# A weave that keeps TensorE's tile shape, and RWKV state products in 64-column form

## Chip and metric

The kernel runs on one core of one Trainium2 chip. The metric is device time in microseconds, the median of several runs. TensorE (PE) does the matrix products, VectorE (DVE), ScalarE (ACT) and GpSimd (POOL) the rest; SP issues most DMAs.

## What is computed

One decoder layer on 2048 tokens of width 1024. Half of the channels go through 8 RWKV-7 heads, a linear recurrence with a 64×64 state per head, half through 8 heads of dilated attention with three patterns (window 128, 512, 2048 at dilation 1, 4, 16). Their outputs are joined, projected, normalised, and go through a mixture of experts. The change is in the part that does RWKV and attention:

```
def step(state, inp):
    r_t, w_t, k_t, v_t, a_t, b_t = inp
    sa = einsum('bhvk,bhk->bhv', state, a_t)
    state = state * w_t + sa[..., None] * b_t + v_t[..., None] * k_t
    y_t = einsum('bhvk,bhk->bhv', state, r_t)
    return state, y_t
...
for window, dil in ((128, 1), (512, 4), (2048, 16)):
    o, l = dilated_branch(q, k, v, rel_bias, window, dil)
...
mix = concatenate([y_rwkv, y_att], -1) @ w_o
```

## The kernel before

The stages follow one another: `project` (input projections and the RWKV inputs), `mixers` (RWKV and attention), `mix_out` (output projection, first norm, router), then the experts. Neighbouring stages overlap at their edges.

In `mixers`, RWKV works in chunks of 128 tokens, two chunks and two heads (one pair, number u) at a time: 16 rounds, each with two pairs i = 0, 1. A round has four parts. `rwkv_front` multiplies triangles (L650, row tiles of 64 rows), cuts out 16×16 blocks, sends them through DRAM to another layout, inverts them on VectorE in 15 steps (L691, L692), sends them back, and GpSimd spreads them into the tile U (L703). `rwkv_inverse` doubles the inverse: products in 128×128 (L742, L748), 32×32 (L756, L766) and 64×64 tiles (L774, L778, L788), then WF (L797). `rwkv_state` makes L822, L834, L849, L858 (128×64 tiles), and then for each chunk c the new state (L875: MK·vt, L877: E·st, both full 128×128 products, of which only the two 64×64 diagonal blocks are kept) and the output (L886 in 128×64 tiles, L888 in 128×128).

Attention runs 12 passes (4 head pairs × 3 patterns) of 16 blocks, dealt to three streams. A block makes scores (L1066 with two key blocks, L1069 with one), adds bias and takes the extreme on VectorE (L1079, L1082), exponentials on ScalarE (L1085), transposes on TensorE (L1091), copies them out (L1095, L1097), and multiplies by V (L1105, 128×64 tiles). When a head pair's three patterns are done, `attn_combine` writes their statistics to DRAM, reads them back in another layout, makes factors, writes and reads these, scales and adds the three outputs (L1213, L1160) and writes y (L1217). `heads(0)` of `mix_out` then loads y (L1313).

All of these are generators, eight and more streams. They yield what they are about to do: an engine and an estimated time (`_pe(430)`), or None where they wait for another stream. `weave` keeps a clock for each engine and for each stream, finds the streams' possible starts, and takes, among those within SLACK = 100 ns of the first, one that `late()` names as being in a hurry, then the lowest number:

```
first = min(starts)[0]
hurry = late()
t, i = min((x for x in starts if x[0] <= first + SLACK), key=lambda x: (x[1] not in hurry, x[1]))
```

So the weave sets the order in which the program is written. In this kernel that is not yet the order on the engines: the recording layer's own scheduler orders each engine's instructions again, except inside `manual_schedule`, where the named engine keeps the order as written. `project` and `mix_out` do that for TensorE, `mixers` does not. At run time every engine takes its instructions in its fixed order.

A matmul has a tile shape, rows × columns of the array that it uses; the profile writes it as 128\*128, 64\*128, 128\*64, 64\*64, 32\*32. An fp32 matmul shows as two records (passes), a transpose and an fp32r matmul as one.

Of the kernel before, what the change touches and what calls it, by code (L numbers as in the profile page):

```python
# [12 lines left out]
AF = mybir.ActivationFunctionType  # L13
# [5 lines left out]
P = 128  # L19
# [37 lines left out]
SLACK = 100.0  # L57
# [5 lines left out]
FRONTS = 2  # L63
HEAD = 10
LATENCY = 100.0
CDEC = math.exp(-0.5)
NEG = -1e30
PATTERNS = (1, 4, 16)
# [48 lines left out]


def _act(n):
    return "ACT", 190 + 0.56 * n  # L120


def _dve(n):
    return "DVE", 60 + 1.06 * n


def _pool(n):
    return "POOL", 100 + 2.2 * n


def _pe(ns):
    return "PE", ns


def _wait(ns):
    return "DMA", ns


def weave(streams, late=lambda: ()):

    clock, now = {}, 0.0
    ready = [0.0] * len(streams)
    pend = [next(g, False) for g in streams]
    while True:
        starts = []
        for i, g in enumerate(streams):
            if pend[i] is None:
                pend[i] = next(g, False)  # L150
                if pend[i]:
                    ready[i] = max(ready[i], now)
            if pend[i]:
                starts.append((max(clock.get(pend[i][0], 0.0), ready[i]), i))
        if not starts:
            assert not any(x is None for x in pend)
            return
        first = min(starts)[0]
        hurry = late()
        t, i = min((x for x in starts if x[0] <= first + SLACK), key=lambda x: (x[1] not in hurry, x[1]))  # L160
        eng, ns = pend[i]
        if eng != "DMA":
            clock[eng] = t + ns
        ready[i] = now = t + ns + LATENCY
        pend[i] = next(streams[i], False)


class K:
# [483 lines left out]
    def rwkv_front(self, n, pps, last):  # L652

        nc, kp = self.nc, self.rf
# [4 lines left out]
        self.busy = True  # L659
        C, Dg = T("C", [P, 2, 4, 32], 1), T("Dg", [P, 2, 4, 16], 1)  # L660
        AB = T("AB", [P, 2, 2, 2, P], ROUNDS)
        yield _pe(900)
        pa = [self.rps[0].tile([P, BT], F32, name="ps0", tag="ps0").rearrange("p (a c s) -> p a c s", a=2, c=2) for _ in range(2)]
        for i, pp in enumerate(pps):
            self.triangles([pa[h][:, i] for h in range(2)], pp, 0)
# [40 lines left out]
    def rwkv_inverse(self, i, pp):  # L706
# [6 lines left out]
            yield None  # L713
        AB, ta = pp["AB"], pp["ta"]
        AW = T("AW", [P, 2, 2, 192])
        yield _pe(500)
        pa = [ps()[:, 0:2 * P].rearrange("p (c s) -> p c s", c=2) for _ in range(2)]
        self.triangles(pa, pp, 1)
        for h in range(2):
# [28 lines left out]
            mm(p2[:, h, c], X[:, h, c], t1[:, h, c], start=True, stop=True)  # L748
        yield _dve(4 * P)
        nc.vector.copy_predicated(U4, self.mask("lv16", 4), p2.rearrange("p h c s -> p (h c) s"))  # L750
        yield _pe(430)
        halves = [(slice(d, d + 32), slice(d + 32, d + 64)) for d in (0, 64)]
        p1 = ps().rearrange("p (h c s) -> p h c s", h=2, c=2)
        for r1, r2 in halves:
# [4 lines left out]
        yield _act(240)  # L759
        for r1, r2 in halves:  # L760
            nc.scalar.copy(t1[r1, :, :, 0:32], p1[r1, :, :, 0:32])
        yield _pe(430)
        p2 = ps().rearrange("p (h c s) -> p h c s", h=2, c=2)
        for r1, r2 in halves:
            for h, c in pairs:
# [2 lines left out]
        for r1, r2 in halves:  # L768
            nc.scalar.copy(U[r1, :, :, r2], p2[r1, :, :, 0:32])
        lo, hi = slice(0, 64), slice(64, 128)  # L770
        yield _pe(250)
        px = ps().rearrange("p (h c s) -> p h c s", h=2, c=2)
        for h, c in pairs:
            nc.tensor.transpose(px[0:64, h, c, 0:64], U[lo, h, c, lo], self.c("eye")[lo, lo])  # L774
        yield _pe(460)
        p1 = ps().rearrange("p (h c s) -> p h c s", h=2, c=2)
        for h, c in pairs:
            mm(p1[lo, h, c, lo], AB[hi, h, c, lo], U[hi, h, c, hi], start=True, stop=True)  # L778
# [3 lines left out]
        yield _act(256)  # L782
        t6 = t1[lo, :, :, lo]
        nc.scalar.copy(t6, p1[lo, :, :, lo])
        yield _pe(460)
        p2 = ps().rearrange("p (h c s) -> p h c s", h=2, c=2)
        for h, c in pairs:
            mm(p2[lo, h, c, lo], X6[:, h, c], t6[:, h, c], start=True, stop=True)  # L788
# [14 lines left out]
    def rwkv_state(self, i, u, q, pp):  # L803
# [13 lines left out]
        yield _pe(950)  # L817
# [36 lines left out]
        yield _pe(700)  # L854
# [12 lines left out]
        for c in range(2):  # L867
            first = q == 0 and c == 0
            last = q == 7 and c == 1
            st, after = (self.state[u][(c + n) % 2] for n in range(2))  # L870
            if not last:
                yield _pe(224 if first else 448)
                pn = ps()[:, 0:P]

                mm(pn, MK[:, c], vt[:, c], start=True, stop=first)  # L875
                if not first:
                    mm(pn, E[:, c], st, start=False, stop=True)  # L877
                yield _act(64)
                rho = self.rho[:, u, q + c, 1 - c:2 - c]
                nc.scalar.activation(after[H[0], H[0]], pn[H[0], H[0]], AF.Copy, scale=rho[H[0]])  # L880
                yield _dve(64)
                nc.vector.tensor_scalar_mul(after[H[1], H[1]], pn[H[1], H[1]], rho[H[1]])
            yield _pe(640)
            py = ps()[:, 0:P]
            for h in range(2):
                mm(py[H[h]], vt[:, c, H[h]], MJ[:, h, c], start=True, stop=first)  # L886
            if not first:
                mm(py, st, Q[:, c], start=False, stop=True)  # L888
            yield _act(128)
            nc.scalar.copy(yt[:, col[c]], py)  # L890
        nc.sync.dma_start(self.y[u * P:(u + 1) * P, q * 2 * P:(q + 1) * 2 * P], yt)
# [2 lines left out]
    def mixers(self, attention=True):  # L894
# [12 lines left out]
        def fronts(s):  # L907
            for n in range(s, len(rounds), FRONTS):
                if n in begun:
                    yield from begun[n]  # L910
                    continue
                while n >= ROUNDS and not all("done" in pp for pp in pps[n - ROUNDS]):
                    yield None
                load(n)
                yield _wait(2500)
                yield from self.rwkv_front(n, pps[n], pps[n - 1])

        def inverses(i):
            for n in range(len(rounds)):
                yield from self.rwkv_inverse(i, pps[n][i])  # L920

        def states(i):
            for n, (q, u) in enumerate(rounds):
                yield from self.rwkv_state(i, u + i, q, pps[n][i])
                self.steps[0] += 1

        with ExitStack() as es:
            att = []
            self.rwkv_setup(es)
            self.busy = False  # L930
# [12 lines left out]
            def late():  # L943

                return range(4 + FRONTS, 8 + FRONTS) if self.steps[1] < (self.steps[0] + HEAD) * PACE else (4 + FRONTS,)

            weave([states(0), states(1), inverses(0), inverses(1), *(fronts(s) for s in range(FRONTS)), *att], late)


    def attn_bias(self, tile, bank):  # L950
# [24 lines left out]
    def attn_streams(self):  # L975
# [71 lines left out]
        def blocks(s, k):  # L1047
            hp, n = passes[k]
            for blk in range((s - k) % 3, 16, 3):
# [50 lines left out]
                yield _pe(550 if two else 275)  # L1100
                o = po[:, at % 2]
                for b in kb:
                    vb = V[:, prev if b == 0 else blk]
# [889 lines left out]
```

## Time and profile before

| | |
|---|---|
| median of 3 runs | 3265.83 us (3265.79 to 3274.77) |
| the profiled execution | 3262.19 us, its span 3260.4 us |
| busy share of the span | PE 90%, DVE 65%, ACT 47%, POOL 21% |
| mean granted TensorE clock | 0.934 |
| HBM | 163 GB/s over the span |

The profile is of one execution. PE's ends are modelled, so the start of the next instruction tells more than an end. The mixers take about 806 to 1815 us of the span.

### The profile page before, as it was taken

The numbers are of one execution on the slowest core, as the hardware profiler recorded it, in microseconds if no ns is written. First come the engines' busy times: TensorE is split into PE (matmuls) and PEld (weight loads), VectorE is DVE, ScalarE is ACT, GpSimd is POOL, SyncE is SP. The second block draws the span as 40 slices with busy tenths as digits, with TensorE's granted clock in tenths as the row PEclk, the third lists the DMA queues.
The fourth block names the chain that finished last, engine by engine and source line by source line (L and its number), as shares of the span: only waits on it lengthen the run. The fifth ranks groups of instructions, "written<-read, shape, count | busy, mean of one in ns | idle before, by whom it ended". The sixth has DMA issues, their size and how long they took to land. (4 is left out here: it accounts for less than half of the span.)

```text
span 3260.4 us, 49197 instructions
## 1 busy us (share of the span) xinstructions
PE 2938.1 (90%) x16686; PEld 2343.0 (72%) x16687; DVE 2118.0 (65%) x4730; ACT 1529.3 (47%) x3650; POOL 675.4 (21%) x682
## 2 busy tenths in 40 slices
PE   7989888999798999998998799899999999998880
PEld 6666777777676777777786577788777777776660
DVE  4997333786654766655757688653577777766756
ACT  3434212554444544543543333311477777765642
POOL 0442000344100211111202122223011111112216
PEclk9999999999898988998897999999999999999985
DMA  5213433788615335234214453243599999987846
GB/s 172 74 59 99 107 81 80 215 273 267 139 55 127 94 74 129 72 95 104 75 31 130 144 183 123 97 138 89 181 298 322 326 301 324 315 296 220 293 129 209
DMA packets 364061, 533.04 MB, mean 163 GB/s; under 512 B 92376, under 2 KB 204640, under 8 KB 363792
## 3 DMA queue, kind: packets, MB, share of 16 engines
q1 hardware_dynamic: 330144, 459.09, 44.1%
q0 software_dynamic: 14496, 45.93, 6.0%
q10 hardware_dynamic: 19168, 24.86, 3.1%
q8 instruction: 133, 2.18, 0.3%
q14 instruction: 120, 0.98, 0.1%
HBM read 402.27 MB, written 128.06 MB: 163 GB/s over the span
## 5 line engine op out<-in xcount | busy, mean ns | idle before, releaser
L1708 DVE TENSOR_TENSOR wl<-raw,wh 128x512 fp32r<-128x512 f32 x768 | 478.3, 681 | 88.4 <-ACT wh L1707 87.7
L1707 ACT CAST wh<-raw 128x512 fp32r<-128x512 f32 x768 | 417.3, 620 | 13.2 <-DMA raw<-in_w_up_dram 12.1
L198 PE MATMUL ps<-xh,wh 128*128 128x512 f32 x640 | 262.6, 410 | 1.1 <-ACT xh L322 1.0
L199 PE MATMUL ps<-xl,wh 128*128 128x512 f32 x640 | 258.7, 404 | 1.2 <-DVE xl L323 1.2
L200 PE MATMUL ps<-xh,wl 128*128 128x512 f32 x640 | 258.2, 403 | 0.0
L1085 ACT ACTIVATE pe<-pe,ms 128x256 f32<-128x256 f32 (+1 forms) x384 | 174.8, 457 | 144.0 <-DVE ms L1082 133.0
L1837 POOL DMA_INDIRECT acc<-ysb,ix x48 | 95.8, 1996 | 623.0 <-ACT ysb L1836 403.0
L198 PE MATMUL pe<-wh,XX 128*128 128x512 f32 x480 | 199.8, 416 | 3.8 <-ACT wh L1707 3.8
L199 PE MATMUL pe<-wl,XX 128*128 128x512 f32 x480 | 192.0, 400 | 2.6 <-DVE wl L1708 2.6
L200 PE MATMUL pe<-wh,XX 128*128 128x512 f32 x480 | 190.9, 398 | 0.0
L198 PEld LDWEIGHTS ps<-xh,wh 128*128 128x128 f32 x640 | 124.7, 195 | 34.6 <-issue 2.6
L199 PEld LDWEIGHTS ps<-xl,wh 128*128 128x128 f32 x640 | 124.7, 195 | 30.1 <-DVE xl L323 2.4
L200 PEld LDWEIGHTS ps<-xh,wl 128*128 128x128 f32 x640 | 124.1, 194 | 29.5
L1091 PE MATMUL pl<-eye,pe 128*128 128x128 f32 x600 | 126.3, 299 | 10.7 <-ACT pe L1085 9.6
L1066 PE MATMUL pl<-KK,Q 128*128 128x256 f32 x432 | 115.4, 393 | 15.6 <-DMA KK<-ks 8.0
L198 PE MATMUL pb<-gh,XH 128*128 128x512 f32 x320 | 126.1, 394 | 0.0
L199 PE MATMUL pb<-gl,XH 128*128 128x512 f32 x320 | 125.2, 391 | 0.0
L1752 PE MATMUL pe<-wh,XX 128*128 128x512 f32 x288 | 120.1, 417 | 5.4 <-ACT wh L1707 5.4
L200 PE MATMUL pb<-gh,XL 128*128 128x512 f32 x320 | 124.9, 390 | 0.0
L1105 PE MATMUL po<-pe,V 128*64 128x128 f32 x1200 | 119.4, 300 | 3.6 <-DVE O L1117 3.2
L1753 PE MATMUL pe<-wl,XX 128*128 128x512 f32 x288 | 118.8, 413 | 2.9 <-DVE wl L1708 2.9
L1082 DVE CUSTOM_DVE_ANT_0 pe<-pl,bias 128x256 f32<-128x256 f32 x216 | 82.6, 418 | 59.7 <-PE pl L1066 37.4
(418 smaller groups left out, 7627.5 us busy)
## 6 DMA issues: line engine op xcount, KB each, us to landing
raw<-in_w_gate_dram SPq DMA_DIRECT2D x128, 512.0 KB
raw<-in_w_up_dram SPq DMA_DIRECT2D x128, 512.0 KB
raw<-in_w_down_dram SPq DMA_DIRECT2D x128, 512.0 KB
pk<-pk SPq DMA_DIRECT2D x32, 512.0 KB
pk_t<-pk SPq DMA_DIRECT2D x32, 512.0 KB
KK<-ks SPq DMA_DIRECT2D x64, 256.0 KB
wr<-in_w_in_dram SPq DMA_DIRECT2D x48, 256.0 KB
rkk<-rkk SPq DMA_DIRECT2D x32, 384.0 KB
```

Of the source, the lines that this page charges most:

```text
L198: mm(out, lh, rh, start=first, stop=False)
L199: mm(out, lh, rl, start=False, stop=False)
L200: mm(out, ll, rh, start=False, stop=last)
L1066: mm(pl[:, h], q, toks(KK[:, m, h], n, prev, 2), start=m == 0, stop=m == 1)
L1085: nc.scalar.activation(pe[:, h, w], pe[:, h, w], AF.Exp, bias=m_[h], scale=-1.0, accum_out=s_[h])
L1091: nc.tensor.transpose(pt[:, h, b], pe[:, h, b * P:(b + 1) * P], self.c("eye"))
L1105: mm(o[h * 64:(h + 1) * 64, j], vb[:, h * 64:(h + 1) * 64], tt[:, h, b], start=b == kb[0], stop=b == 1)
L1707: nc.scalar.copy(wh[:, c], raw[:, c])
L1708: nc.vector.tensor_tensor(out=wl[:, c], in0=raw[:, c], in1=wh.bitcast(F32)[:, c], op=ALU.subtract)
L1752: mm(ps, L[:, 0:P], wh, start=first, stop=False)
L1753: mm(ps, L[:, 0:P], wl, start=False, stop=last)
L1837: nc.gpsimd.indirect_dma_start(out=self.acc, out_offset=bass.IndirectOffsetOnAxis(ap=ix[0:r, e, b:b + 1], axis=0), in_=ysb[0:r], in_offset ...
```

## The change

The pieces now also say the tile shape that they use (`_pe(430, 32)`; 128 is the full array, 1 stands for 64×128, 2 for 128×64). The weave remembers the shape in use, counts 190 ns for a change, lets a TensorE piece of the same shape be taken up to KEEP = 600 ns after the first possible start, and prefers such pieces to a hurry. The weave runs inside `manual_schedule` for TensorE. And four products of `rwkv_state` are written as pairs on 128×64 tiles: the state in two 64-column halves (pn is 64 columns wide), the output's Q product by halves of its rows.

```diff
-    return "ACT", 190 + 0.56 * n
+    return "ACT", 190 + 0.56 * n, 0
...
-def _pe(ns):
-    return "PE", ns
+def _pe(ns, mode=128):
+    return "PE", ns, mode
...
 def weave(streams, late=lambda: ()):
-    clock, now = {}, 0.0
+    clock, now, tile_ = {}, 0.0, 128
...
-        t, i = min((x for x in starts if x[0] <= first + SLACK), key=lambda x: (x[1] not in hurry, x[1]))
-        eng, ns = pend[i]
+        other = lambda i: pend[i][0] == "PE" and pend[i][2] != tile_
+        t, i = min((x for x in starts if x[0] <= first + (SLACK if other(x[1]) or pend[x[1]][0] != "PE" else KEEP)), key=lambda x: (other(x[1]), x[1] not in hurry, x[1]))
+        eng, ns, mode = pend[i]
+        if eng == "PE":
+            ns += CHANGE * other(i)
+            tile_ = mode
...
             if not last:
-                yield _pe(224 if first else 448)
-                pn = ps()[:, 0:P]
-                mm(pn, MK[:, c], vt[:, c], start=True, stop=first)
+                yield _pe(110 if first else 220, 2)
+                pn = ps()[:, 0:64]
+                for h in range(2):
+                    mm(pn[H[h]], MK[:, c, H[h]], vt[:, c, H[h]], start=True, stop=first)
                 if not first:
-                    mm(pn, E[:, c], st, start=False, stop=True)
+                    for h in range(2):
+                        mm(pn[H[h]], E[:, c, H[h]], st[:, H[h]], start=False, stop=True)
                 yield _act(64)
...
-            yield _pe(640)
+            yield _pe(220 if first else 440, 2)
             py = ps()[:, 0:P]
             for h in range(2):
                 mm(py[H[h]], vt[:, c, H[h]], MJ[:, h, c], start=True, stop=first)
             if not first:
-                mm(py, st, Q[:, c], start=False, stop=True)
+                for h in range(2):
+                    mm(py[H[h]], st[:, H[h]], Q[:, c], start=False, stop=True)
...
-            weave([states(0), states(1), inverses(0), inverses(1), *(fronts(s) for s in range(FRONTS)), *att], late)
+            with self.tc.manual_schedule(engines={mybir.EngineType.PE}):
+                weave([states(0), states(1), inverses(0), inverses(1), *(fronts(s) for s in range(FRONTS)), *att], late)
```

Lines move by 8 to 12 in the changed code: L650 becomes L658, L742 L750, L875 and L877 become L884 and L887, L886 and L888 become L896 and L899, L1066 and L1069 become L1078 and L1081, L1091 becomes L1103, L1105 L1117, L1217 L1229.

Three places in TensorE's order. First the opening of the stage, up to the first product with an inverse U. In the kernel before (the rows just ahead of it; L1091 transposes, L1105 attention products, L1066 scores):

```order
L1105 MATMUL po<-pe_7672,V 64x128 x4
L1066 MATMUL pl_7736<-KK,Q 128x256 x4
L1105 MATMUL po<-pe_7661,V 64x128 x4
L1066 MATMUL pl_7781<-KK,Q 128x256 x4
L1091 MATMUL pl_7789<-eye,pe_7741 128x128 x2
L742 MATMUL ps_7582<-U_7219,AB 128x128 x4
```

and in the changed one (L1117 products, L1078 scores, L1103 transposes, L750 the product with U):

```order
L1117 MATMUL po<-pe_7349,V 64x128 x2
L1117 MATMUL po<-pe_7356,V 64x128 x4
L1117 MATMUL po<-pe_7369,V 64x128 x4
L1078 MATMUL pl_7519<-KK,Q 128x256 x4
L1078 MATMUL pl_7526<-KK,Q 128x256 x4
L1078 MATMUL pl_7533<-KK,Q 128x256 x4
L750 MATMUL ps_7541<-U_7219,AB 128x128 x4
L1103 MATMUL pl_7548<-eye,pe_7524 128x128 x4
```

Of the attention products (L1105, now L1117), 42 stood ahead of the first product with U, and 10 do now: the three rows here are all of them.

Second a state update in the middle. Before (L858 gives E and Q; L875, L877 the state; L886, L888 the output):

```order
L1091 MATMUL pl_12533<-eye,pe_12338 128x128 x4
L875 MATMUL ps_11623<-vt_11263,MK_11201 128x128
L877 MATMUL ps_11623<-S_7124,E_7132 128x128
L849 MATMUL ps_11879<-RB_11333,WF_11678 128x192 x2
L849 MATMUL ps_11884<-RB_11333,WF_11678 128x192 x2
L742 MATMUL ps_11627<-U_11549,AB 128x128 x4
L1105 MATMUL po<-pe_12355,V 64x128 x4
L1066 MATMUL pl_12619<-KK,Q 128x256 x4
L1066 MATMUL pl_12635<-KK,Q 128x256 x3
L886 MATMUL ps_11638<-MJ_11200,vt_11263 64x128 x2
L888 MATMUL ps_11638<-Q_11612,S_7124 128x128
L858 MATMUL ps_11904<-RB_11333,WF_11678 64x192 x4
```

and changed:

```order
L866 MATMUL ps_12292<-RB_11776,WF_12207 64x192 x4
L866 MATMUL ps_12301<-RB_11839,WF_12215 64x192 x4
L884 MATMUL ps_12309<-vt_11903,MK_11778 64x64 x2
L887 MATMUL ps_12309<-S_7128,E_7132 64x64 x2
L1117 MATMUL po<-pe_12112,V 64x128 x2
L884 MATMUL ps_12323<-vt_11934,MK_11841 64x64 x2
L887 MATMUL ps_12323<-S_7130,E_7133 64x64 x2
L896 MATMUL ps_12329<-MJ_11777,vt_11903 64x128 x2
L899 MATMUL ps_12329<-Q_12306,S_7128 64x128 x2
L884 MATMUL ps_12338<-vt_11903,MK_11778 64x64 x2
L887 MATMUL ps_12338<-S_7129,E_7132 64x64 x2
L896 MATMUL ps_12344<-MJ_11840,vt_11934 64x128 x2
```

All twelve rows of the second piece have one tile shape, 128×64; the first piece changes shape five times.

Third the end of the stage. Before, the last attention product and the start of the RWKV matmuls that follow it, 227 in number with the first ones of `mix_out` among them:

```order
L766 MATMUL ps_15680<-t_15546,X_15545 32x32 x8
L1105 MATMUL po<-pe_17036,V 64x128 x4
L774 MATMUL ps_16114<-eye,U_15603 64x64 x4
L778 MATMUL ps_16120<-U_15603,AB 64x64 x4
L774 MATMUL ps_15701<-eye,U_15543 64x64 x4
```

Changed, the last RWKV matmuls and the start of the 234 attention matmuls that follow them:

```order
L896 MATMUL ps_16745<-MJ_16354,vt_16488 64x128 x2
L899 MATMUL ps_16745<-Q_16715,S_7131 64x128 x2
L1081 MATMUL pl_16752<-KK,Q 128x256 x2
L1103 MATMUL pl_16757<-eye,pe_16656 128x128 x2
L1117 MATMUL po<-pe_16656,V 64x128 x2
```

Attention ended first and now ends last; the combine of the last head pair follows it in both.

## Rows read from the trace of the kernel before

**Rows 1.** busy time by stretch: us, busy us by engine, granted clock, DMA

```profile
806.00:1717.00 911.00, 854.95 (x6853) 689.98 (x6851) 546.27 (x2029) 431.50 (x1488) 135.79 (x250) 0.92 0.38 92
1717.00:1815.00 98.00, 72.94 (x436) 57.09 (x436) 65.78 (x138) 33.46 (x81) 23.64 (x15) 0.72 0.56 157
```

**Rows 2.** waits of TensorE from 810 to 1717 us, longest in total

```profile
PE ps L858 <- DVE AW L721: 14.6, 2, 9.2
```

**Rows 3.** timeline of TensorE: start us, us, engine, line, operation, out<-in, form, records

```profile
1644.05 1.16 PE L742 MATMUL ps<-U,AB 128*128 128x128 f32 x8
1645.14 0.44 PE L886 MATMUL ps<-MJ,vt 128*64 128x128 f32 x4
...
1701.19 0.44 PE L1105 MATMUL po<-pe,V 128*64 128x128 f32 x4
1701.56 0.66 PE L834 MATMUL ps<-eye,pk_t 128*128 128x128 f32 x4
...
1702.64 0.66 PE L1105 MATMUL po<-pe,V 128*64 128x128 f32 x8
1703.23 1.71 PE L650 MATMUL ps<-pk_t 64*128 64x128 f32 x16
```

**Rows 4.** timeline of TensorE around one state update

```profile
1640.12 0.39 PE L875 MATMUL ps<-vt,MK 128*128 128x128 f32 x2
1640.34 0.39 PE L877 MATMUL ps<-S,E 128*128 128x128 f32 x2
1640.66 0.44 PE L1105 MATMUL po<-pe,V 128*64 128x128 f32 x4
1641.03 1.31 PE L1066 MATMUL pl<-KK,Q 128*128 128x256 f32 x4
1642.27 0.43 PE L1105 MATMUL po<-pe,V 128*64 128x128 f32 x2
```

**Rows 5.** timeline of the weight loads there

```profile
1640.23 0.30 PEld L877 LDWEIGHTS ps<-S,E 128*128 128x128 f32 x2
1640.66 0.20 PEld L1105 LDWEIGHTS po<-pe,V 128*64 128x64 f32 x4
```

**Rows 6.** timeline of the opening, TensorE, then GpSimd (POOL)

```profile
843.91 0.66 PE L1105 MATMUL po<-pe,V 128*64 128x128 f32 x8
...
850.33 0.44 PE L1091 MATMUL pl<-eye,pe 128*128 128x128 f32 x2 [3.71 <-ACT pe L1085]
...
871.89 0.66 PE L1105 MATMUL po<-pe,V 128*64 128x128 f32 x8
...
874.21 1.06 PE L742 MATMUL ps<-U,AB 128*128 128x128 f32 x8
...
872.76 2.51 POOL L703 TENSOR_TENSOR U<-ct,Vc 128x512 f32<-128x512 f32 x2 [1.87 <-DMA Vc<-inv]
```

**Rows 7.** timeline of VectorE and ScalarE between scores and products

```profile
1702.43 0.42 DVE L1082 CUSTOM_DVE_ANT_0 pe<-pl,bias 128x256 f32<-128x256 f32 x1
...
1703.55 0.51 ACT L1085 ACTIVATE pe<-pe,ms 128x256 f32<-128x256 f32 x1
...
1707.75 0.59 ACT L1095 COPY pe<-pl 128x512 f32<-128x512 f32 x1 [0.93 <-PE pl L1091]
```

**Rows 8.** timeline of the end: TensorE, SP's DMA issues, TensorE

```profile
1716.97 0.66 PE L1105 MATMUL po<-pe,V 128*64 128x128 f32 x8 [0.28 <-ACT pe L1095]
...
1767.72 5.66 SPq L1217 DMA_DIRECT2D y<-O  x2
1773.42 0.43 SPq L1313 DMA_DIRECT2D y<-y  x1
...
1815.41 0.58 PE L198 MATMUL pa<-woh,YH 128*128 128x512 f32 x1
```

**Rows 9.** busy time by stretch, two neighbours

```profile
1151.00:1157.90 6.90, 6.90 (x41) 5.73 (x40) 4.27 (x16) 2.95 (x14) 1.20 (x3) 1.00 0.14 20
1157.96:1171.61 13.65, 13.65 (x60) 11.05 (x60) 6.07 (x18) 3.55 (x13) 4.35 (x11) 0.50 0.24 69
```

More of the change, by code (lines that the diff above doesn't have):

```diff
@@ L65 @@
 LATENCY = 100.0
+CHANGE = 190.0
+KEEP = 600.0
 CDEC = math.exp(-0.5)
@@ L119, in _act @@
 def _act(n):
-    return "ACT", 190 + 0.56 * n
+    return "ACT", 190 + 0.56 * n, 0
 def _dve(n):
-    return "DVE", 60 + 1.06 * n
+    return "DVE", 60 + 1.06 * n, 0
 def _pool(n):
-    return "POOL", 100 + 2.2 * n
-def _pe(ns):
-    return "PE", ns
+    return "POOL", 100 + 2.2 * n, 0
+def _pe(ns, mode=128):
+    return "PE", ns, mode
 def _wait(ns):
-    return "DMA", ns
+    return "DMA", ns, 0
 def weave(streams, late=lambda: ()):
-    clock, now = {}, 0.0
+    clock, now, tile_ = {}, 0.0, 128
     ready = [0.0] * len(streams)
@@ L661, in rwkv_front @@
         AB = T("AB", [P, 2, 2, 2, P], ROUNDS)
-        yield _pe(900)
+        yield _pe(900, 1)
         pa = [self.rps[0].tile([P, BT], F32, name="ps0", tag="ps0").rearrange("p (a c s) -> p a c s", a=2, c=2) for _ in range(2)]
@@ L715, in rwkv_inverse @@
         AW = T("AW", [P, 2, 2, 192])
-        yield _pe(500)
+        yield _pe(500, 1)
         pa = [ps()[:, 0:2 * P].rearrange("p (c s) -> p c s", c=2) for _ in range(2)]
@@ L750, in rwkv_inverse @@
         nc.vector.copy_predicated(U4, self.mask("lv16", 4), p2.rearrange("p h c s -> p (h c) s"))
-        yield _pe(430)
+        yield _pe(430, 32)
         halves = [(slice(d, d + 32), slice(d + 32, d + 64)) for d in (0, 64)]
@@ L761, in rwkv_inverse @@
             nc.scalar.copy(t1[r1, :, :, 0:32], p1[r1, :, :, 0:32])
-        yield _pe(430)
+        yield _pe(430, 32)
         p2 = ps().rearrange("p (h c s) -> p h c s", h=2, c=2)
@@ L770, in rwkv_inverse @@
         lo, hi = slice(0, 64), slice(64, 128)
-        yield _pe(250)
+        yield _pe(250, 64)
         px = ps().rearrange("p (h c s) -> p h c s", h=2, c=2)
@@ L774, in rwkv_inverse @@
             nc.tensor.transpose(px[0:64, h, c, 0:64], U[lo, h, c, lo], self.c("eye")[lo, lo])
-        yield _pe(460)
+        yield _pe(460, 64)
         p1 = ps().rearrange("p (h c s) -> p h c s", h=2, c=2)
@@ L784, in rwkv_inverse @@
         nc.scalar.copy(t6, p1[lo, :, :, lo])
-        yield _pe(460)
+        yield _pe(460, 64)
         p2 = ps().rearrange("p (h c s) -> p h c s", h=2, c=2)
@@ L816, in rwkv_state @@
         MJ, MK = T("MJ", [P, 2, 2, P]), T("MK", [P, 2, P])
-        yield _pe(950)
+        yield _pe(950, 1)
         prs = [ps().rearrange("p (c k s) -> p c k s", c=2, k=2) for _ in range(2)]
@@ L853, in rwkv_state @@
             nc.vector.tensor_tensor(out=MK[:, :, H[h]], in0=pm[h][:, :, P:192], in1=MK[:, :, H[h]], op=ALU.add)
-        yield _pe(700)
+        yield _pe(700, 2)
         pq = ps()[:, 0:384].rearrange("p (c s) -> p c s", s=192)
@@ L871, in rwkv_state @@
             if not last:
-                yield _pe(224 if first else 448)
-                pn = ps()[:, 0:P]
-                mm(pn, MK[:, c], vt[:, c], start=True, stop=first)
+                yield _pe(110 if first else 220, 2)
+                pn = ps()[:, 0:64]
+                for h in range(2):
+                    mm(pn[H[h]], MK[:, c, H[h]], vt[:, c, H[h]], start=True, stop=first)
                 if not first:
-                    mm(pn, E[:, c], st, start=False, stop=True)
+                    for h in range(2):
+                        mm(pn[H[h]], E[:, c, H[h]], st[:, H[h]], start=False, stop=True)
                 yield _act(64)
                 rho = self.rho[:, u, q + c, 1 - c:2 - c]
-                nc.scalar.activation(after[H[0], H[0]], pn[H[0], H[0]], AF.Copy, scale=rho[H[0]])
+                nc.scalar.activation(after[H[0], H[0]], pn[H[0]], AF.Copy, scale=rho[H[0]])
                 yield _dve(64)
-                nc.vector.tensor_scalar_mul(after[H[1], H[1]], pn[H[1], H[1]], rho[H[1]])
-            yield _pe(640)
+                nc.vector.tensor_scalar_mul(after[H[1], H[1]], pn[H[1]], rho[H[1]])
+            yield _pe(220 if first else 440, 2)
             py = ps()[:, 0:P]
@@ L1099, in blocks @@
                     yield None
-                yield _pe(550 if two else 275)
+                yield _pe(550 if two else 275, 2)
                 o = po[:, at % 2]
```

## The prediction

> **What bounds the kernel now.** I read the page's busy shares first, and they put TensorE far ahead of every other engine. The change touches one stage, the mixers, so I then read the busy time by stretch [rows 1]. The mixers hold TensorE from about 806 us, where the first RWKV matmuls come in, to 1815 us, where the output projection flows. That is two stretches. Until 1717 us, where the last attention product runs, TensorE is busy for 854.95 of 911 us at a granted clock of 0.92. In the 98 us after it, it is busy for 72.94 us at 0.72. The first stretch is bound by TensorE's own issue, the second by latency. The waits of TensorE in the first stretch add up to some 55 us, the largest group 14.6 in two waits [rows 2], so most of it is not waiting. What does it spend on?
>
> The timeline of TensorE answers. The product line L1105 (128\*64 tiles) runs with 4 records, and the next line starts 0.37 us later; with 8 records the next starts 0.59 us later [rows 3]. Four records more cost 0.22 us, 0.055 each, so a section of one tile shape has a fixed cost of 0.37 − 0.22 = 0.15 us, paid at the change of shape. Where the shape stays (L877 after L875), two records take 0.22 us with no such gap; when L1105 follows L877, it starts 0.32 us after L877 instead of 0.22 [rows 4]. So 0.10 of the 0.15 us lies ahead of the new section, 0.05 in its first weight load.
>
> **The change, part by part.**
>
> *Fewer changes of shape.* Counted along TensorE's order as built, from the first RWKV matmul to the last of the stage: 991 changes of tile shape before, 338 now. In the stretch before either order's end piece (below) it is 950 against 316. 634 fewer × 0.15 us = **−95 us**. Nothing hides this cost, since TensorE is the engine that is waited for. The low bound is the gap alone, 0.10 × 634 = 63 us. The high one comes from L742: eight records and 1.09 us to the next line [rows 3], 8 × 0.11 and 0.21 more, so 133 us. I take 0.15, as L1105 is the commonest section. [...] The weight load of L1105 starts with its matmul, at 1640.66 us, 0.43 us behind the first load for L877, which stood 0.11 us ahead of its own matmul [rows 4, 5]; across a change the pull-ahead is not there, and the measurement decides for 0.15.
>
> *State products.* The new state of a chunk was one 128-column product MK·vt and one E·st (L875, L877), four records of 0.11 us [rows 4]. Now each is two 64-column products side by side on 128\*64 tiles (L884, L887). No row shows that form. The nearest, L1105 with 128 columns, takes 0.055 us a record with two side by side [rows 3]; with half the columns, half of that, and twice the records: 8 × 0.027 = 0.22 us for 0.44. 56 such pairs: **−12 us**. If the records do not shrink with their columns, 8 × 0.055 = 0.44 us and nothing is won, which is the other end. The output's second product (L888, now L899) keeps 2 × 0.11 us as 4 × 0.055; splitting it saves only changes, counted above.
>
> *The opening.* The order is now the weave's own, and TensorE can't pass a wait. The first RWKV product that needs the inverse U (L742, now L750) ran at 874.21 us, right behind the U that GpSimd wrote from 872.76 us [rows 6]. Ahead of it stood 42 attention products; now there are 10. U comes through three DMA round trips and is not made earlier by this change. So TensorE has 32 products, eight blocks of two keys, less to fill that wait: a block is 4 scores, 4 transposes and 4 products, about 0.11 to 0.13 us each, plus three changes, 1.8 us. **+15 us** (0 if U comes that much earlier, 20 with the clock at half for part of it).
>
> *Shorter distances.* Pieces of one shape now stand together, so scores, transposes and products of three attention streams come in threes and a block's own next step stands closer behind. From a block's scores to its transposes, VectorE and ScalarE need from 1702.43 to 1704.06 us [rows 7]; I count against 1.5 us, since the first head's transposes need not wait for the second. From transposes to products it is a copy of 0.59 us [rows 7] and the hand-over on either side, an estimated 0.85. I added up the work that stands between in the new order, with the durations above: it is under 1.5 us ahead of the transposes for 22 of 192 blocks, and under 0.85 us ahead of the products for 43. The missing time sums to 29 us; in the old order, by the same count, to 2. A wait of one stream covers that of its neighbours, but a crowded ScalarE lengthens the need. **+20 us** (0 to 60).
>
> *The end.* Before, attention ended first: its last product at 1716.97 us, its combine (statistics out to memory and back, factors out and back) beside the last RWKV round, the last y written from 1767.72, the first load of the next stage at 1773.42, the projection flowing at 1815.41 us [rows 8]. Now RWKV ends first, and 234 attention matmuls in 26 blocks stand behind it, and behind these the combine with nothing beside it. The 26 blocks have 41 us of matmuls and changes, with the strided scores at (1.24 − 0.15)/4 = 0.27 us [rows 4]; nearly alone, from the products at 843.91 to those at 871.89 us, eight more blocks of two keys took 28 us, 3.5 us each [rows 6]. 12 of the 26 have two keys, 14 have one and half the work: 12 × 3.5 + 14 × 1.75 = 66 us. The combine and first loads took 98 us from the last product; 56 of it up to 1773.42, in which VectorE and SP also served RWKV, so I take 40, and 26 of the 42 behind it: 66. Together 132 us for 98: **+34 us** (9, if the blocks run at 41, to 60). The RWKV work that stood there, 45 us with its changes, is about what the attention rest is, so the sums match.
>
> Sum against the profiled execution, 3262.19 us (span 3260.4): −95 − 12 + 15 + 20 + 34 = −38, **3224 us**. The median of the three runs is 3265.83, 3.6 us above that execution; I leave the sum where it is.
>
> **The rivals.**
>
> *The covers hold.* TensorE stays fed as before and the end is no longer than now: 3262 − 107 = 3155 us. For it: DVE at 546 and ACT at 432 of 911 us [rows 1] have room; the U of all later rounds now stands further behind its triangles. Against it: the end piece is plain in the order. Chance 0.16.
>
> *The fixed order waits.* This is the one on the other side. TensorE in the weave's order waits at scores → transposes → products because the three streams arrive together, and nothing may pass. It decides where the added wait per block exceeds (38 + 20)/192 = 0.30 us; at 0.5 us, a third of the chain of [rows 7], it is 96 us instead of 20, so 3224 + 76 = 3300 us. For it: at 850.33 TensorE waited 3.71 us for ScalarE with attention nearly alone [rows 6]. Against it: between 874 and 1717 such waits are rare [rows 2]. Chance 0.18.
>
> *The clock falls more.* [...] Chance 0.06.
>
> *It does nothing.* The changes of shape are not what TensorE spends on, since something else paces it: 3262 us. Against it: [rows 3, 4]. Chance 0.05.
>
> **How the numbers follow.** My forecast has 0.55, and its own range goes from 3180 to 3255. The range takes in the covers case with changes at 0.15, the bounds of the end, and most of the waiting case: 3155 to 3295. A measurement of this kernel tells 0.3% (10 us) from no change. Faster by more: 0.55 + 0.16 = 0.71. Within: 0.06 + 0.05 = 0.11. Slower: 0.18.
>
> **What would show it.** Right: TensorE's records between 874 us and RWKV's end in about 95 us less time; lines L884 to L899 as one section; a wait of over 15 us ahead of the first L750; a stretch of about 65 us with attention lines alone, then about 65 us nearly empty of matmuls. Wrong: if sections with the same records still cost 0.15 us where the shape stays; if waits at L1103 and L1117 add up to over 60 us (second rival); if the end piece is under 100 us (first rival).

## The result, and the profile after

The changed kernel takes 3375.31 us (median of 4 runs, 3371.83 to 3381.03), the kernel before beside it 3265.81 us: ratio 1.0332, 95% interval 1.0310 to 1.0354. By that ratio it is slower by 108 us. The forecast was 3224 us, the range 3155 to 3295. The profiled execution took 3371.83 us, its span is 3370.0 us.

The busy time by stretch of the changed kernel answers to [rows 1] (us, then busy us of PE, its weight loads, DVE, ACT, POOL, then the granted clock, the DMA share and GB/s). The stretches are RWKV to its end, the attention rest, and the combine with the first loads of the next stage.

```profile
806.00:1773.00 967.00, 776.64 (x7303) 669.37 (x7301) 541.32 (x1977) 414.17 (x1408) 138.16 (x253) 0.85 0.36 87
1773.00:1853.00 80.00, 58.90 (x318) 39.34 (x316) 30.04 (x133) 35.48 (x134) 0.24 (x1) 0.71 0.21 59
1853.00:1925.00 72.00, 13.56 (x33) 8.09 (x30) 34.53 (x58) 16.41 (x27) 18.02 (x12) 0.51 0.60 163
```

Ahead of RWKV's end TensorE now idles for 967 − 777 = 190 us where it idled for 56, and the granted clock is 0.85 for 0.92.

To compare whole stages, I cut each execution at 806 us and at 1470 us before the end of its span; what follows the second cut is the experts and the end of the projection. Two rows give that stretch, for the kernel before and then for the changed one:

```profile
806.00:1790.40 984.40, 917.22 (x7244) 741.02 (x7243) 597.75 (x2139) 458.69 (x1551) 155.34 (x260) 0.90 0.39 96
```

```profile
806.00:1900.00 1094.00, 836.42 (x7618) 708.96 (x7616) 591.38 (x2144) 458.55 (x1551) 153.53 (x261) 0.82 0.36 89
```

By these cuts the two stretches differ by as much as the spans, 1094.0 − 984.4 = 109.6 us. That nothing is lost behind them is seen at the last product of the output projection, which stands 1191 us ahead of the end of the span before and 1189 after. I split the stretch in three: **idle** is the length less PE's busy time; the **half-clock cost** is half of PE's busy time inside the stretches granted 0.50 (before 170 us busy in 198 at 0.50, after 268 in 390); **work** is the rest, busy time as at full clock (in the kernel before, eight records of L822 take 1.08 us to the next line at 1100.98 us, granted 1.00, and 2.01 us at 826.89, granted 0.50). Before: 67 idle, 85 half clock, 832 work. After: 258, 134, 702. So work fell by 130 us, more than the 107 of the forecast, idle time rose by 190 and the half-clock cost by 49.

The work that went is to be seen where the 128\*64 sections now run into each other (timeline of TensorE, answering to [rows 3, 4]):

```profile
1396.51 0.64 PE L1117 MATMUL po<-pe,V 128*64 128x128 f32 x8
1396.95 0.31 PE L884 MATMUL ps<-vt,MK 128*64 128x64 f32 x4
...
1398.05 0.48 PE L896 MATMUL ps<-MJ,vt 128*64 128x128 f32 x4
1398.27 0.48 PE L899 MATMUL ps<-Q,S 128*64 128x128 f32 x4
```

Eight records take 0.44 us to the next line, four 0.22, with nothing between: 0.055 a record, and no 0.15 us.

The idle time is to be seen in TensorE's costliest groups from 806 to 1925 us (busy us, mean ns, idle before them and what ended it):

```profile
L1103 PE MATMUL pl<-eye,pe 128*128 128x128 f32 x600 | 119.2, 317 | 28.3 <-ACT pe L1097 23.9 <-DVE ms L1094 1.7 <-DVE Dg L686 0.8
L1117 PE MATMUL po<-pe,V 128*64 128x128 f32 x1200 | 109.6, 307 | 65.1 <-ACT pe L1107 18.8 <-DVE O L1129 18.3 <-DVE O L1131 15.1
...
L658 PE MATMUL ps<-pk_t 64*128 64x128 f32 x512 | 53.5, 305 | 31.3 <-DVE MJ L835 13.3 <-DVE MK L861 4.9 <-DVE AW L729 4.5
```

Attention's transposes and products, L1103 and L1117, wait 93 us, 72 of it ahead of RWKV's end; RWKV's first product L658 waits 31 us, nearly all of it for VectorE, whose lines L835, L861 and L729 read the ps tiles that TensorE wrote before. The longest of these waits, in the timeline of TensorE, VectorE and ScalarE:

```profile
1031.42 0.66 PE L1117 MATMUL po<-pe,V 128*64 128x128 f32 x8
1042.95 0.19 DVE L1172 TENSOR_TENSOR mn<-stt 128x32 f32<-128x32 f32 x1 [14.89 <-DMA stt<-stat]
...
1043.84 0.28 ACT L1181 ACTIVATE f<-f 128x96 f32<-128x96 f32 x1 [12.48 <-DVE f L1172]
1044.03 0.57 ACT L1107 COPY pe<-pl 128x512 f32<-128x512 f32 x1
1044.65 1.12 PE L1117 MATMUL po<-pe,V 128*64 128x128 f32 x8 [12.58 <-ACT pe L1107]
```

VectorE waits 14.9 us for a DMA of the combine, ScalarE 12.5 us for VectorE, the copy L1107 starts 0.19 us behind ScalarE's L1181, and TensorE waits 12.6 us for the copy. None of the three engines has a record inside its wait, so this one fault stops all three. TensorE's records stand in the order as built: at the opening 20 of L1117 from 854.04 us, 12 of L1078 from 855.28, then L750 after a wait of 12.70 us, with L1103's transposes behind it.

This fault is not what the change brought. The kernel before has it too:

```profile
1049.24 0.19 DVE L1160 TENSOR_TENSOR mn<-stt 128x32 f32<-128x32 f32 x1 [11.87 <-DMA stt<-stat]
...
1049.99 0.80 PE L877 MATMUL ps<-S,E 128*128 128x128 f32 x2 [7.37 <-DVE E L862]
```

Up to the end of the first of the two, attention or RWKV, TensorE's waits at these stops add up to 22 us before (7.4, 5.4 and 9.2; the last two are the 14.6 of [rows 2]) and to 21 us now (12.6 and 8.5). What is new are other and mostly shorter waits. From 900 us, behind the opening, TensorE waits 37 us to 1717 in the kernel before and 148 us to RWKV's end now. Two rows of the waits in that stretch now (us in total, times, longest), then the one that answers to them before:

```profile
PE po L1117 <- DVE O L1129: 18.3, 12, 8.6
...
PE po L1117 <- DVE O L1131: 12.2, 10, 3.2
```

```profile
PE po L1105 <- DVE O L1117: 2.8, 2, 2.0
```

L1129, L1131 and L1133 copy attention's finished products out of PSUM, and the next products wait for that: 33 us for 3. With the stops at the combine left out, these waits rise by 112 us, in the main: +30 here, +18 where attention's transposes and products wait for ScalarE, and +65 where RWKV's lines wait for VectorE (+49) and ScalarE (+16).

The end answers to [rows 8] (TensorE, SP's DMA issues, TensorE):

```profile
1852.41 1.12 PE L1117 MATMUL po<-pe,V 128*64 128x128 f32 x8 [0.73 <-ACT pe L1107]
...
1893.37 4.98 SPq L1229 DMA_DIRECT2D y<-O  x2
1898.40 0.43 SPq L1325 DMA_DIRECT2D y<-y  x1
...
1901.61 0.76 PE L1334 MATMUL pa<-y,ct 128*128 128x256 f32 x1 [47.73 <-DMA y<-y]
```

The combine now has nothing beside it: TensorE waits 47.7 us in one piece.

### The profile page after: what moved, and what is told of

The parts are those of the page before. It is cut to its first block, busy times and chain, and to the rows that moved or that the text cites. A ratio compares the mean times of both kernels' runs of the same rounds, so it can differ in the third digit from the quotient of the medians.

```text
span 3370.0 us, 49843 instructions
## 1 busy us (share of the span) xinstructions
PE 2863.6 (85%) x17038; PEld 2314.6 (69%) x17039; DVE 2111.3 (63%) x4730; ACT 1529.9 (45%) x3650; POOL 673.1 (20%) x682
## 5 line engine op out<-in xcount | busy, mean ns | idle before, releaser
L1117 PE MATMUL po<-pe,V 128*64 128x128 f32 x1200 | 109.6, 307 | 65.1 <-ACT pe L1107 18.8
L1103 PE MATMUL pl<-eye,pe 128*128 128x128 f32 x600 | 119.2, 317 | 28.3 <-ACT pe L1097 23.9
L1117 PEld LDWEIGHTS po<-pe,V 128*64 128x64 f32 x1200 | 71.1, 148 | 90.9 <-ACT pe L1107 24.6
L1103 PEld LDWEIGHTS pl<-eye,pe 128*128 128x128 f32 x600 | 79.4, 157 | 55.5 <-ACT pe L1097 50.0
```

The costliest lines, as they stand in the source:

```text
L1103: nc.tensor.transpose(pt[:, h, b], pe[:, h, b * P:(b + 1) * P], self.c("eye"))
L1117: mm(o[h * 64:(h + 1) * 64, j], vb[:, h * 64:(h + 1) * 64], tt[:, h, b], start=b == kb[0], stop=b == 1)
```

## The experiments

The change has three parts: TensorE's fixed order, the preference for the shape, and the 64-column products. Theory A: the fixed order itself costs, since TensorE can't pass a late result, and attention ends last. Theory B: the preference costs, since it bunches pieces. The table has all runs, sorted by what they hold. The time is a ratio to the kernel before beside it (its medians there are 3265.8 to 3274.8 us), "us" is that ratio on 3266 us, and the last three columns split the profiled execution as above. That is one execution, which can lie well off the median: e12's 18 us under it, e11's 12 under, e14's 11 over.

| run | order | preference | products | other | ratio (95%) | us | idle | half clock | work |
|---|---|---|---|---|---|---|---|---|---|
| before | | | | | 1 | 0 | 67 | 85 | 832 |
| changed | x | x | x | | 1.0332 (1.0310 to 1.0354) | +108 | 258 | 134 | 702 |
| e1 | x | | | | 1.0334 (1.0265 to 1.0403) | +109 | 222 | 111 | 770 |
| e2 | | x | x | | 0.9944 (0.9913 to 0.9974) | −18 | 76 | 93 | 807 |
| e3 | | | x | | 0.9933 (0.9905 to 0.9960) | −22 | 70 | 88 | 807 |
| e4 | x | | x | | 1.0444 (1.0377 to 1.0512) | +145 | 239 | 135 | 761 |
| e5 | x | x | x | HEAD 20 | 1.0141 (1.0106 to 1.0175) | +46 | 224 | 104 | 711 |
| e6 | x | x | x | LATENCY 600 | 1.0141 (1.0103 to 1.0179) | +46 | 251 | 107 | 694 |
| e7 | x | x | x | both | 0.9967 (0.9943 to 0.9991) | −11 | 183 | 92 | 708 |
| e8 | x | x | x | KEEP 100 | 1.0241 (1.0204 to 1.0278) | +79 | 240 | 128 | 709 |
| e9 | x | | | as e7 | 1.0126 (1.0081 to 1.0171) | +41 | 186 | 83 | 765 |
| e10 | x | x | x | LATENCY 600, HEAD 22, KEEP 300 | 0.9999 (0.9972 to 1.0027) | 0 | 180 | 97 | 709 |
| e11 | | x | x | HEAD 5 | 1.0024 (0.9998 to 1.0049) | +8 | 68 | 107 | 812 |
| e12 | x | x | x | row halves apart | 1.0284 (1.0248 to 1.0320) | +93 | 240 | 112 | 720 |
| e13 | | | x | L822 alternates | 0.9895 (0.9861 to 0.9929) | −34 | 97 | 82 | 784 |
| e14 | | | x | L822 and L650 alternate | 0.9931 (0.9911 to 0.9951) | −23 | 102 | 98 | 785 |

### The order alone

```diff
+            with self.tc.manual_schedule(engines={mybir.EngineType.PE}):
                 weave([...
```

> The kernel before, with TensorE kept in the weave's order and nothing else changed. Theory A (the fixed order itself costs: TensorE can't pass a late result, and attention now ends last): slower than before by 70 to 160 us, so 3335 to 3425 us, with over 100 us more of TensorE waits between 806 us and the end of RWKV, and attention ending after RWKV. Theory B (the preference for the tile shape costs, by bunching the pieces): within 35 us of before (the end alone), 3255 to 3300 us, waits as before.

3382.13 us, ratio 1.0334: the whole loss, without any preference. The stage's row and TensorE's groups (lines stand one further than in the kernel before, from the weave on):

```profile
806.00:1909.60 1103.60, 881.64 (x7260) 702.65 (x7259) 594.25 (x2145) 464.63 (x1553) 153.91 (x261) 0.85 0.36 89
```

```profile
L1106 PE MATMUL po<-pe,V 128*64 128x128 f32 x1200 | 123.7, 324 | 43.8 <-ACT pe L1096 11.0 <-DVE O L1120 10.2 <-DVE O L1118 9.8
L1092 PE MATMUL pl<-eye,pe 128*128 128x128 f32 x600 | 118.4, 314 | 21.4 <-ACT pe L1086 18.9 <-DVE ms L1083 1.3 <-DVE pe L1080 0.5
...
L650 PE MATMUL ps<-pk_t 64*128 64x128 f32 x512 | 58.6, 310 | 34.5 <-DVE MK L853 17.2 <-DVE Q L865 4.0 <-ACT MK L840 3.4
```

The same places wait, 65 us at attention's products and transposes (41 of it ahead of RWKV's end) and 35 at L650, and attention ends 84 us after RWKV here too. Idle time ahead of RWKV's end is 150 us for 56, so 94 more and not the over 100 expected. Still Theory A holds, and that attention ends last comes from the order, not from the preference.

### Without the order

```diff
-            with self.tc.manual_schedule(engines={mybir.EngineType.PE}):
-                weave([...
+            weave([...
```

> The changed kernel without the fixed order: the preference and the 64-column products stay, TensorE's order is the scheduler's again. Theory A: the loss is gone, 3245 to 3270 us (12 us won by the products, little by the preference, as the scheduler reorders). Theory B: most of the loss stays, over 3320 us.

3256.59 us: the loss is gone. The preference does nothing there: with it 0.9944, without it (the next run) 0.9933, with 1095 and 1092 changes of shape in TensorE's order, for 1125 in the kernel before (counted over all of the stage's instructions, so more than the 991 of the prediction).

### The 64-column products alone

> The kernel before with the four state products written on 128x64 tiles, nothing else. Both theories: the prediction's term of -12 us, so 3254 us; 3266 if the records do not shrink with their columns. Either way the new-state section of 8 records is read from the trace: 0.22 us by the term, 0.44 by its other end.

The edit is the part of the change in `rwkv_state` alone. 3249.66 us, ratio 0.9933, −22 us (31 to 13). The records shrink with their columns (timeline of TensorE in this run; L876 and L879 are the new state):

```profile
1236.80 0.34 PE L876 MATMUL ps<-vt,MK 128*64 128x64 f32 x4
1236.96 0.29 PE L879 MATMUL ps<-S,E 128*64 128x64 f32 x4
1237.08 0.39 PE L888 MATMUL ps<-MJ,vt 128*64 128x128 f32 x4
```

Eight records take 0.28 us to the next line, L879 alone 0.12, where four took 0.44 [rows 4]; the first four come behind a change of shape. 56 times that 0.16 us is 9 of the 12 us of the term. The rest of the 22 has 33 fewer changes of shape in it, some 4 us; what else is in it stays open.

### The order without the preference

```diff
-        t, i = min((x for x in starts if x[0] <= first + (SLACK if other(x[1]) or pend[x[1]][0] != "PE" else KEEP)), key=lambda x: (other(x[1]), x[1] not in hurry, x[1]))
+        t, i = min((x for x in starts if x[0] <= first + SLACK), key=lambda x: (x[1] not in hurry, x[1]))
```

> The changed kernel with the choice of before in the weave (no preference for the shape; the fixed order and the 64-column products stay). The preference is worth -95 us of shape changes by the prediction. Theory A: this is as slow as the fixed order alone less 12 us, 3325 to 3410 us, and TensorE's work in full-speed time is some 65 us more than in the changed kernel. Theory B: without the preference the loss goes, 3245 to 3285 us.

3418.08 us, ratio 1.0444, the slowest of all, 8 us beyond Theory A's range. So the preference wins 37 us (145 − 108, give or take some 23 by the intervals) under the fixed order. It has 472 changes of shape for 929, and the work is 761 − 702 = 59 us less: 0.13 us a change. Idle time takes 19 of that back. The run also shows what the products do here: against the order alone (3382.13 us) they cost 36 us, where without the order they won 22. The work does fall, by 9 us, but idle time rises by 17 and the half-clock cost by 24. So the loss of 108 us is 109 for the order, 36 for the products under it, and 37 back by the preference.

### The end and the distances

HEAD decides how far attention is hurried ahead of RWKV; LATENCY is what the weave adds to every result's time before the next step of its stream may start.

```diff
-HEAD = 10
+HEAD = 20
```

> The changed kernel with HEAD = 20 for 10: attention is in a hurry ten rounds' steps longer, and its last product now has 208 RWKV matmul instructions behind it in TensorE's order (the kernel before had 225) where the changed kernel has RWKV ended and 80 attention products left. If the end costs what the trace of the changed kernel shows (152 us from the end of RWKV to the output projection, 54 over the 98 of before), 3375 - 54 = 3320 us, and the idle time of TensorE before it stays near 190 us. If the attention rest only moves its waits forward, 3350 to 3380 us.

```diff
-LATENCY = 100.0
+LATENCY = 600.0
```

> The changed kernel with LATENCY = 600 for 100 ns: the weave takes every result to be ready 0.5 us later, so it puts more other work between a piece and the next one of its stream; 574 changes of shape for 472. Theory A in its narrow form (the fixed order waits since the weave's result times are earlier than the chip's): TensorE's idle time up to the end of RWKV falls from 190 us to about 100 us, for about 13 us more of shape changes, 3375 - 77 = 3298 us. If the waits come from something the distance doesn't mend (buffers, DMAs, the half clock): 3360 to 3390 us.

Both edits:

> Both edits of the two runs ahead: 3375 - 54 - 77 = 3244 us if the end and the distance add up and are all of the loss; 3300 us or more if the fixed order waits for other reasons.

HEAD = 20: 3321.70 us, 62 us won; TensorE's idle time up to attention's end is 976 − 770 = 206 us, so of the idle time only the end's was mended; the half-clock cost is 30 us less as well (busy time by stretch):

```profile
806.00:1782.00 976.00, 770.26 (x7238) 661.06 (x7237) 558.79 (x2073) 432.47 (x1494) 137.01 (x251) 0.87 0.36 87
1782.00:1874.00 92.00, 59.55 (x425) 47.00 (x426) 51.85 (x97) 32.50 (x75) 20.72 (x14) 0.76 0.57 170
```

LATENCY = 600: 3326.58 us, 62 us won, but not as expected. The idle time up to RWKV's end is 182 us and not 100. Attention's waits halve and others take their place (groups of TensorE to 1857 us, in this run):

```profile
L1103 PE MATMUL pl<-eye,pe 128*128 128x128 f32 x600 | 108.2, 312 | 19.9 <-ACT pe L1097 16.0 <-DVE ms L1094 3.4 <-DVE S L892 0.3
L1117 PE MATMUL po<-pe,V 128*64 128x128 f32 x1200 | 105.6, 310 | 24.1 <-DVE V L700 7.4 <-ACT pe L1107 5.2 <-DVE O L1129 4.1
L1078 PE MATMUL pl<-KK,Q 128*128 128x256 f32 x432 | 102.4, 383 | 20.2 <-DMA KK<-ks 15.0 <-issue 5.2
```

L1103 and L1117 wait 44 us for 93, L1078 20 for 3, now for the loads of the keys. Of the 43 us by which the stage is shorter, 27 are half-clock cost. Both edits together win 119 us (62 + 62 are 124), and the kernel stands at 0.9967: two numbers of the weave win back the whole loss. They do not mend the waits, though (busy time of the run with both, to attention's end):

```profile
806.00:1728.00 922.00, 751.46 (x7248) 654.16 (x7249) 556.51 (x2065) 429.81 (x1497) 136.85 (x251) 0.87 0.38 93
```

TensorE still idles 922 − 751 = 171 us there, against 190 in the changed kernel and 56 before. What comes back is idle time of the end (54 us) and half-clock cost (42). The kernel is level with before since its work is 124 us less, which pays for 116 us more idle time.

### Is it the bunching?

```diff
-KEEP = 600.0
+KEEP = 100.0
```

> The changed kernel with KEEP = 100 for 600 ns: a piece of the shape in use is preferred only among those due within 100 ns; 622 changes of shape for 472. If bunching makes the waits, idle time falls by over 50 us and the time to about 3345 us; if bunching is harmless, 150 changes at 0.13 to 0.15 us are lost: 3395 us.

3354.74 us, 29 us won by the ratio; the profiled executions lie 17 us apart. Idle time falls by 18 us, not by over 50, so bunching makes a small part of the waits at most. And the 150 more changes of shape bring only 7 us more work, 0.05 us a change where the pair above gave 0.13. With the longer distances nothing is won:

```diff
-LATENCY = 100.0
-HEAD = 10
-KEEP = 600.0
+LATENCY = 600.0
+HEAD = 22
+KEEP = 300.0
```

> The changed kernel with LATENCY = 600, HEAD = 22 and KEEP = 300 (724 changes of shape). KEEP = 100 alone won 21 us at LATENCY = 100. If bunching costs also where the distances are longer, 3261 - 20 = 3241 us; if the longer distance had mended that already, 122 more changes at 0.13 us cost 16 us: 3277 us.

3270.55 us, 0.9999 against 0.9967 with KEEP = 600 and HEAD = 20. The work is 709 us for 708, with 122 more changes: here they cost next to nothing.

The kernel before with the order, LATENCY = 600 and HEAD = 20, without preference and products:

> The kernel before with TensorE in the weave's order, LATENCY = 600 and HEAD = 20; no preference for the shape, no 64-column products (937 changes of shape). If distance and end are all that a fixed order needs, they win here what they won in the changed kernel (114 us): 3382 - 114 = 3268 us, level with before. If they win only beside the preference, since it is the preference that closes the distances, 3300 to 3340 us.

3309.98 us: the two numbers win 68 us of 109 here, against 119 in the changed kernel. A fixed order needs more than these two, and the expectation of 3268 us was wrong. From here to the run with both edits, preference and products are worth 52 us. How that divides is not shown: the products won 22 us without the order and cost 36 under it.

### The end without the order

> The run without the fixed order, with HEAD = 5: attention now ends 245 TensorE instructions ahead of the last state product instead of 598. Its own trace has attention ending at 1665 us and RWKV at 1811, 20 us after the output projection could start. If that early end costs, 3257 - 15 = 3242 us; if the order of the end does not matter there, 3250 to 3260 us.

The edit is HEAD = 5 in the run without the order. 3276.89 us, slower and not faster: so attention's early end at 1665 us shows no cost there. Its idle time is 68 us, its half-clock cost 107 for 93. Why is not known.

### Row halves

By the table, the order alone takes 832 − 770 = 62 us of work away, and 191 fewer changes at 0.13 us are 25. The triangle products L822 and L650 run on 64\*128 row tiles, the upper and the lower 64 rows by turns as the program writes them. The scheduler had put records of one half together: of L822's 195 neighbours 43 alternate in the kernel before, of L650's 176 neighbours 28. Timeline of the kernel before, then with the order alone:

```profile
1100.98 1.16 PE L822 MATMUL ps<-pk_t 64*128 64x128 f32 x8
1102.06 0.33 PE L1091 MATMUL pl<-eye,pe 128*128 128x128 f32 x1
```

```profile
1110.49 1.16 PE L822 MATMUL ps<-pk_t 64*128 64x128 f32 x16
1111.58 0.66 PE L1106 MATMUL po<-pe,V 128*64 128x128 f32 x8
```

Eight records of one half take 1.08 us, sixteen by turns 1.09. Over the stage the two lines lose 39 us of full-clock work under the order.

The changed kernel with the halves apart again:

```diff
-        for c in range(2):
-            for m in range(2):
-                for h in range(2):
+        for h in range(2):
+            for c in range(2):
+                for m in range(2):
                     mm(prs[h][:, c, m], bk[c][H[h], m], rt[c][H[h]], start=True, stop=True)
```

and the loops of `triangles` in the same way.

> The changed kernel with the loops of the triangle products (L658, L830) turned round, so that all records of the upper 64 rows stand ahead of all of the lower 64, as the scheduler had put most of them in the kernel before; all other instructions stay where they are, with as many changes of shape. Theory P (a gain that the prediction did not see: 64*128 products whose row halves alternate run side by side): sections of 16 records take twice their 1.09 us, and the kernel loses 30 to 50 us, 3405 to 3425 us. If the halves do not matter: 3375 us within 10.

3368.60 us, ratio 1.0284: no slower than the changed kernel. A price of the halves is there (L833 is L830 of the changed kernel):

```profile
1135.04 1.71 PE L833 MATMUL ps<-pk_t 64*128 64x128 f32 x16
1137.14 1.79 PE L658 MATMUL ps<-pk_t 64*128 64x128 f32 x16 [0.39 <-DVE MJ L838]
```

Sixteen records now take 1.71 us (1137.14 − 1135.04, less the wait of 0.39), not twice 1.09, and the work rises by 17 us, not by 30 to 50. The time does not rise with it, a sign that TensorE's work no longer sets the pace. Idle time and half-clock cost fall by 17 and 22 us in the profiled execution, but it took 3350.20 us and the other three 3364.61 to 3373.55, so these two falls are not shown for the rest.

Do the halves help where TensorE waits less? The kernel before with the 64-column products and this:

```diff
+        with self.tc.manual_schedule(engines={mybir.EngineType.PE}):
             for c in range(2):
                 for m in range(2):
                     for h in range(2):
                         mm(prs[h][:, c, m], bk[c][H[h], m], rt[c][H[h]], start=True, stop=True)
```

> The kernel before with the 64-column products, and with only the loop of L822 kept in written order, so that its row halves alternate (194 of 196 neighbours, 43 of 195 before); the rest of TensorE's order is the scheduler's. Theory P: 16 records take 1.09 us instead of 8, 32 sections, some 25 us less than the 64-column products alone: 3250 - 25 = 3225 us. If the short kept piece disturbs the scheduler as the whole fixed order did: 3260 us or more.

3242.59 us, ratio 0.9895 (0.9861 to 0.9929): the lowest median of all kernels here, 34 us under the kernel before. Over the products alone (0.9905 to 0.9960) it gains 12 us and not 25, and the intervals overlap, so that gain is not shown. TensorE's groups, for the products alone and for this run:

```profile
L822 PE MATMUL ps<-pk_t 64*128 64x128 f32 x512 | 69.4, 305 | 5.8 <-DVE S L884 5.8
```

```profile
L823 PE MATMUL ps<-pk_t 64*128 64x128 f32 x512 | 51.0, 296 | 1.3 <-DVE S L885 1.3
```

The line is busy 18 us less, and the whole work falls by 23 (807 to 784), as Theory P had it. But idle time rises by 27, and the profiled executions are 2 us apart (3242.75 and 3240.90): here too work that is taken away comes back as waits. With L650 kept in order as well:

> As the run ahead, with the triangles of L650 kept in written order too (177 of 181 neighbours alternate, 28 of 176 before). Theory P: 14 us less again by the work of L650 under the fixed order, 3211 us. If the earlier end of attention or a disturbed order takes it back: 3225 to 3260 us.

3251.66 us: nothing more, perhaps less. Attention ends earlier still, and RWKV at 1819 us for 1802; what takes the gain back is not settled.

## Why the prediction was wrong

**Fewer changes and products (−107).** Right in kind, and −130 as work, but the nearness is partly luck. The triangle products L658 and L830 alone have 45 us less full-clock work than before (126 to 81), some of it by their row halves (17 us of work come back with the halves apart), which the prediction did not look at: no count of changes of shape holds them. That leaves 85 us for changes and products, for the forecast 107. A price of 0.15 us for every change is not borne out: the run without the preference gives 0.13, e8 0.05, and e10 against e7 next to nothing. Why it differs is open.

**The opening (+15).** About right: from 806 to 900 us TensorE idles 40 us for 19, so +21. The wait for U is 12.70 us at 869.67, a little under the 15 that the prediction named as its sign.

```profile
869.67 2.08 PE L750 MATMUL ps<-U,AB 128*128 128x128 f32 x8 [12.70 <-POOL U L711]
```

**Shorter distances (+20).** This is the step that failed. It took two of attention's hand-overs, scores to transposes and transposes to products, held them against an undisturbed chain [rows 7], and put every other hand-over at nothing. The two that it counted came to about what it said: +18 us of waits for ScalarE. What it left out came to +95: attention's products wait for VectorE to copy earlier ones out of PSUM (+30), and RWKV's lines wait for VectorE and ScalarE (+65). So idle time ahead of the end piece rose by 134 us (190 − 56) for the 35 of this step and the opening. It put the waits down to pieces bunched by their shape, too. Under the order alone, with the old choice, that idle time is already 150 us, and KEEP = 100 takes 15 of the 190 away (964 − 789 = 175). The waits come with the fixed order. Why VectorE and ScalarE come late at these hand-overs no run takes apart.

**The end (+34).** Right in kind and too low: 80 + 72 = 152 us for the forecast 66 + 66, against 98 before, so +54. The run with HEAD = 20 gives 62 us back.

**The clock.** Not in the sum, and +49 us. No run shows what a clock that falls more costs by itself, for which the prediction gave a chance of 0.06; the runs showed the half-clock cost of each kernel, 82 to 135 us. The clock stands at half with TensorE fully busy too, for 13.65 us in one piece [rows 9]. Long runs of transposes are not borne out as the cause here: runs of ten or more in a row are 14 in the changed kernel and 3 in the one without the preference (e4), and the half-clock cost is 134 and 135 us. It goes with idle time in most runs, but not in all (e9: 186 us idle and 83, e11: 68 and 107), and its cause stays open.

**The rival that came true** is the second, with a chance of 0.18: the fixed order waits. Its own sign was over 60 us at L1103 and L1117; it is 93 us, close to its price of 96, but only in part of the kind that it priced: 39 of the 93 are waits for VectorE's copies (L1129, L1131, L1133) and 12.6 is the stop at the combine, which the kernel before has too. It gave 3300 us, since it left RWKV's waits, the clock and the rest of the end out. "Between 874 and 1717 such waits are rare" spoke against it in the prediction [rows 2]. That was read from the kernel before, whose order the scheduler had made; it said nothing of a kernel without it, and there lay the misjudged chance.

**The sum.** −130 work, +190 idle, +49 half clock: +109.

## What to carry to other kernels

Taking an engine's order from a scheduler is a change in its own right, to be costed ahead of what it was done for: here it costs 109 us, and the preference that needs it wins 37. When you cost it, go through every hand-over at which the engine could now wait, those of the other streams and of the buffers too, and not only those that the new order makes shorter. Before expecting a gain from less work on an engine, ask if it will still be the one that is waited for; a cheap test is to add work and see if the time moves. And compare with the smallest part of the change: the 64-column products alone gave 0.9933, the best of the fixed orders 0.9967, the whole change 1.0332. That L822 kept in order adds to the products (0.9895) is not clear of the noise.

## What the runs showed of the hardware

On 64\*128 row tiles, 16 records with upper and lower rows by turns took 1.09 us in the run with the order alone, and 32 took 2.06 us in the changed kernel (L830 at 1102.86 us, up to a wait of 0.23), where the granted clock was 1.00. Eight records of one half took 1.08 us in the kernel before, at 1.00 as well. With the changed kernel's loops turned round and nothing else, 16 records took 1.71 us. The granted clock was 0.50 for 198 us of the stage before and 390 after; no run separates the reason.
